# A fourth block-sum step in the later gate-and-up pairs of a two-layer encoder trunk

## The chip, the cores and the metric

The kernel runs on one core of one Trainium2 chip. The metric is the device time of one execution in microseconds; the median of several runs is compared. The profile is one execution taken by the hardware profiler; its busy times, waits and starts are the basis of all that follows. TensorE is PE in the profile's lines (PEld its weight loads), VectorE is DVE, ScalarE is ACT, GpSimd is POOL and SyncE, which issues most loads, is SP.

## The reference, cut to what matters

The trunk has two layers on 256 tokens of 2048 features, all in float32. Layer 0 mixes tokens by grouped-query attention, layer 1 by a recurrent block (a projection, a short convolution, two gated linear recurrences and an output projection). Each layer ends in the same feed-forward part:

```
x = x + mixer(rmsnorm(x))
x = x + swiglu(rmsnorm(x))
swiglu(h) = (silu(h @ w_gate) * (h @ w_up)) @ w_down     # w_gate, w_up: 2048 x 5632, w_down: 5632 x 2048
```

## The kernel before

**Matmuls in three passes.** Every float32 weight tile is split into two parts, `hi` (a rounded copy, by ScalarE, L141) and `lo` (the rest, by VectorE, L143), and so are the activations. A product is three matmuls: hi x hi, hi x lo, lo x hi. The tokens are the stationary operand (128 at a time), and 512 weight columns stream past them. A half is one load of 512 KB: two blocks of 128 input features by 512 output columns. Loads (`load_half`) use five buffers each for `raw`, `hi` and `lo`.

**Feed-forward order.** The 5632 hidden features of a layer are worked in eleven units of 512, called gate-and-up pairs here: a pair computes 512 columns of gate and of up at the same time. The eleven pairs come in three parts of 3, 4 and 4 (`PARTS`, in blocks of 128); after each part the down projection of its hidden features is added to the token-major residual `x_tok`, in two stages of two groups of 512 columns each. A pair has 2048 / 256 = 8 steps. A plain step loads one half for gate and one for up and does 8 products, 24 matmuls.

**Block-sum steps.** In some steps (`THREE` = 1, 3, 5; in the first pair of a layer 3 and 5) the 2 x 2 block product (two token blocks, two feature blocks, two column groups) is done with seven products, 21 matmuls, instead of eight, in the manner of Strassen and Winograd. It needs sums of weight blocks and of token blocks. `seven_forms` makes those of the weights: one half is loaded and split as always; a second transfer on POOL's queue writes the other half to `sr` and a third adds a part to it in flight (`fetch_next`, two buffers, each chain started when the buffer comes free); `wx` (256 KB, on SP's queue, one buffer) is a fourth. VectorE forms the sums in place (L320, L324, L325), ScalarE casts them (L322, L323, L327) and VectorE makes the low parts (L326, L328, L329). `x_forms` makes the token sums: for the layer's input once per step number (tiles `nf1`, `nf3`, `nf5`), and for the hidden features once per part (`hf0` to `hf2`). Four products go to PSUM tiles of their own (`p1`, `q5`, `q6`, `q7`, pool `pm`, four buffers); after the last block-sum step `merge` combines them into `g` and `u` in SBUF (tiles `fg`, `fu`). The other products go to the four ordinary accumulators (`acc`, four buffers).

**The order in a pair.** `unit_plan` and `pair_plan` write it: up to and including the last block-sum step, gate and up go together step by step; the remaining steps first for gate, then for up. When gate's last product is done, VectorE adds the accumulators to `g` (L848) and ScalarE applies silu; when up's is done, VectorE adds them to `u` (L851) and multiplies (L852). Then `u` is turned from token-major to feature-major: VectorE transposes 32 x 32 blocks (L865), ScalarE makes 16 small copies that put the blocks in place (L871, four calls of `copies`, four copies in each), and one cast (L878) and one subtraction (L879) split the result.

**What sets the order of the work.** TensorE's instructions run in the order written. For the other engines a scheduler of the framework decides, under order rules that the program adds: `in_line` keeps the weight work of ScalarE and of VectorE in the order of loading; `follow` puts one instruction behind another; `not_after` with `settled` says that an instruction must stand before the weight subtraction of the third half from then. The turning is not written out where it arises: its pieces go into a list `owed`, and `settle(n)` takes n pieces out at a given step, up to three at a block-sum step and one or two at a half of a plain one.

**The first gates.** In the recurrent mixer the projection is done in groups of 128 columns, and the gates of a block of 256 features are matmuls put between them by a clock: `later(delay, ...)` runs a piece once `delay` steps have gone by (a step is three matmuls of 256 columns there). `WHEN_FIRST` has the delays for block 0: its four gates at 24, 30, 36 and 42. A gate needs the split convolution output `xs` (L439, L440), reads weights `ghi` and `glo`, and then issues the weight load of the gate four places later (`load_gates`: a load on SP's queue, a cast on ScalarE, a subtraction on POOL).

Of the kernel before, what the change touches and what calls it, by code (L numbers as in the profile page):

```python
# [12 lines left out]
F32 = mybir.dt.float32  # L13
F32R = mybir.dt.float32r
AF = mybir.ActivationFunctionType
ALU = mybir.AluOpType
AX = mybir.AxisListType

P = 128
S = 256  # L20
D = 2048
KT = D // P
# [4 lines left out]
DFF = 5632  # L27
PARTS = [12, 16, 16]
THREE, TWO, SHORT = (1, 3, 5), (2, 5), 6
READY = 6  # L30
FIRST_STEPS = (0, 1, 2, 4, 3, 6, 5, 7)
HALF = 8
# [2 lines left out]
FOUR = WIDE // P  # L35
# [14 lines left out]
VALUES = (62, 98)  # L50
GATE_BUFS = 4
WHEN = (18, 25, 32, 39, 42, 46, 50, 54, 58, 60, 62, 64, 66, 70, 74)
WHEN_FIRST = (24, 30, 36, 42) + WHEN[4:]
WHEN_LAST = (5, 9, 13, 17, 19, 20, 21, 24, 24, 25, 26, 27, 33, 39, 39)

PK = {}
# [14 lines left out]
def trunk(ctx, tc, w, out):  # L71
    nc = tc.nc
    act, dve, pool, pe, sync = nc.scalar, nc.vector, nc.gpsimd, nc.tensor, nc.sync
# [13 lines left out]
    def nm(s):  # L87
        uid[0] += 1
        return f"{s}_{uid[0]}"
# [28 lines left out]
    def not_after(i, ahead=3, eng="dve"):  # L118
        due.setdefault((taken[0] + ahead, eng), []).append(i)
# [36 lines left out]
        return [(n, (0, 1)) for n in steps[:together]] + [(n, (j,)) for j in range(2) for n in steps[together:]]  # L156

    def unit_seven(i):
        return THREE[1:] if i == 0 else THREE

    def unit_plan(i):
        steps = range(KT // 2) if i else FIRST_STEPS
        return pair_plan(steps, 1 + steps.index(unit_seven(i)[-1]))

    def down_plan(n, alone):
# [36 lines left out]
    steps = range(KT // 2)  # L202
# [88 lines left out]
    owed = []  # L291

    def settle(n=1):
        while owed and n:
            owed.pop(0)()
            n -= 1
# [49 lines left out]
    def project_pair(xs, forms, plan, middle, done, ready=None):  # L346
        banks = [[], []]
        begun = set()

        def bank(j, a):  # L350
            while len(banks[j]) <= a:
                banks[j].append(new_acc())
            return banks[j][a]

        def product(acc, x, wt, last=False):
            for i, (a, b) in enumerate(((x[0], wt[0]), (x[0], wt[1]), (x[1], wt[0]))):
                pe.matmul(acc, a, b, start=id(acc) not in begun, stop=last and i == 2)  # L357
                begun.add(id(acc))
            step()
            step()  # L360

        def tokens(k, a):
            return [xs[k][:, o + a * P : o + (a + 1) * P] for o in (0, S)]

        seven = [n for n, cols in plan if n in forms]
        for i, (n, cols) in enumerate(plan):
            if n in forms:
                s1, s2, s3, s4 = forms[n]
                b11, b21, t3, b22, t1, t2, t4 = seven_forms()
                settle(3)  # L370
                if n == seven[0]:
                    p1, q6, q5, q7 = (ps_m.tile([P, WIDE], F32, tag="pm", name=nm("pm")) for _ in range(4))
                last = n == seven[-1]
                product(p1, tokens(2 * n, 0), b11, last)
                product(bank(0, 0), tokens(2 * n + 1, 0), b21)
                product(bank(1, 0), s4, b22)
                product(q7, s3, t3, last)
                product(q5, s1, t1, last)
                product(q6, s2, t2, last)
                product(bank(0, 1), tokens(2 * n + 1, 1), t4)  # L380
                if last:
                    middle(p1, q5, q6, q7)
                continue
            if len(cols) == 1 and i and len(plan[i - 1][1]) == 2:
                settle(-1)
                if ready:
                    ready()
            end = n == plan[-1][0]
            for j in cols:
                half()  # L390
                if i:
                    settle(2 if len(owed) > 6 else 1)
                hi, lo = (flat(t) for t in newest["tiles"])
                for a in range(2):
                    for k in range(2):
                        product(bank(j, a), tokens(2 * n + k, a), (hi[:, k, :], lo[:, k, :]), end and k == 1)
                if end:
                    done(j, banks[j])

    def merge(p1, q5, q6, q7):  # L400
        g, u = (fp[1].tile([P, 2, WIDE], F32, tag=t, name=nm(t), bufs=1) for t in ("fg", "fu"))
        act.copy(g[:, 0, :], p1)
        dve.tensor_tensor(g[:, 1, :], q6, g[:, 0, :], ALU.subtract)
        dve.tensor_tensor(u[:, 0, :], q5, g[:, 1, :], ALU.add)
        dve.tensor_tensor(g[:, 1, :], q7, g[:, 1, :], ALU.subtract)
        dve.tensor_tensor(u[:, 1, :], u[:, 0, :], q7, ALU.subtract)
        return g, u

    def three(o, hi, lo, x, start, stop):
# [56 lines left out]
    class Norm:  # L466
# [18 lines left out]
        def add(self, c):  # L485
            last = c == NCOL - 1
            parts = []
            fields = {}

            def first():  # L490
                for a in range(2):
                    act.activation(tmp("nj", (P, WIDE), mybir.dt.bfloat16, 1), x_tok[:, a, c, :], AF.Square, accum_out=self.sums[:, a, c : c + 1])
                if last and self.seven:
                    self.finish()
                fields["b"] = fp[0].tile([P, 2, FOUR, P], F32, tag="tb", name=nm("tb"))
                fields["f"] = fp[0].tile([P, 8, FOUR, 32], F32, tag="tf", name=nm("tf"))
                for a in range(2):
                    dve.transpose(fields["b"][:, a, :, :], x_tok[:, a, c, :])

# [50 lines left out]
    fp = []  # L550
# [285 lines left out]
    def ffn(norm, nxt):  # L836
# [4 lines left out]
        def unit(hid, hid_units, forms, parts, i):  # L841
# [19 lines left out]
            kept = {}  # L861

            def transposes():
                kept["b"], kept["f"] = (fp[0].tile([P, 2 * FOUR, P], F32, tag=n, name=nm(n), bufs=1) for n in ("tb", "tf"))
                dve.transpose(kept["b"], got[1])  # L865

            def copies(q):
                b = kept["b"][:].rearrange("p (a i) (k t) -> p a i k t", a=2, k=FOUR)
                f = kept["f"][:].rearrange("p q (k t) -> p q k t", k=FOUR)
                for i in range(4):  # L870
                    n = act.copy(f[32 * i : 32 * i + 32, q::4, :, :], b[32 * q : 32 * q + 32, :, i, :, :])  # L871
                    follow(n, line["act"])

            def split_tiles():
                f = kept["f"][:].rearrange("p q (k t) -> p k q t", k=FOUR)
                h = act_tiles()
                hi, lo = (h[:, :, o : o + S].rearrange("p k (q t) -> p k q t", t=32) for o in (0, S))
                act.copy(hi, f)  # L878
                dve.tensor_tensor(lo, f, hi.bitcast(F32), ALU.subtract)  # L879
                hid.extend(h[:, k, :] for k in range(FOUR))  # L880
                for k, n in enumerate(THREE):
                    if n in down_seven(parts // 2, False) and first <= 2 * n < len(hid):
                        forms[n] = x_forms(hid[2 * n], hid[2 * n + 1], f"hf{k}")

            owed.extend([transposes, *(partial(copies, q) for q in range(4)), split_tiles])

        line.update(act=None, dve=None)
        for p, n in enumerate(PARTS):
# [238 lines left out]
```

## Time and profile before

| | |
|---|---|
| median of 3 runs | 1963.46 us (1961.83 to 1963.49) |
| the profiled execution | 1964.66 us, span 1962.8 us |
| TensorE matmuls | 9641, busy 1955.2 us |
| VectorE busy | 1737.4 us (89%) |
| ScalarE busy | 1357.9 us (69%) |
| GpSimd busy | 233.7 us (12%) |
| loads from device memory | 431.02 MB, 221 GB/s over the span |
| mean granted TensorE clock | 0.998 |

Matmuls overlap in the pipe, so the mean length of one (389 ns for 512 columns) is longer than the distance from one start to the next; the distance is what counts for a sum. Operations of VectorE that follow one another overlap a little too, and there too the distance of starts is the price. A row of the timeline gives start, length, engine, line and operation, and how often; in square brackets stands how long the engine was idle before it and who released it. A row of the chain of waits gives start, length and what ran. A row of the windows gives, for a stretch, each engine's busy time and count, the granted clock, the share of the DMA engines and GB/s.

### The profile page before, as it was taken

What the parts mean: (1) busy time and instruction counts of PE and PEld (TensorE: products, weight loads), DVE (VectorE), ACT (ScalarE), POOL (GpSimd) and SP (SyncE); (2) the same over time, 40 slices, a digit from 0 to 9 for tenths busy, and PEclk for the clock granted to TensorE, in tenths of its full rate; (3) what the DMA queues carried; (4) which work ended last, traced back from release to release, by engine and by line L of the source; (5) the groups of instructions that cost most, each with busy time, mean ns of one, the idle gap of its engine ahead of it and who ended that gap; (6) DMA issues with size and microseconds to landing.
All of it is one profiled execution on the core that took longest, in us unless ns stands there. A gap on an engine that the chain in (4) does not pass through costs nothing.

```text
span 1962.8 us, 27715 instructions
## 1 busy us (share of the span) xinstructions
PE 1955.2 (100%) x9641; PEld 1659.9 (85%) x9641; DVE 1737.4 (89%) x2374; ACT 1357.9 (69%) x2075; POOL 233.7 (12%) x333
## 2 busy tenths in 40 slices
PE   9999999999999999999999999999999999999999
PEld 8888888888888888888899998888888888888887
DVE  6777889999999989999778986999998999989997
ACT  6666767665677556777689986767756776567763
POOL 0011000010011100101034331001101010011010
PEclk9999999999999999999999999999999999999999
DMA  8544667687677876776545556567767777777784
GB/s 333 186 147 138 202 204 240 219 258 246 209 246 242 269 245 214 228 234 232 197 166 184 190 166 209 193 203 243 245 233 239 240 240 255 229 245 236 234 261 163
DMA packets 136364, 434.95 MB, mean 222 GB/s; under 512 B 15264, under 2 KB 16160, under 8 KB 135968
## 3 DMA queue, kind: packets, MB, share of 16 engines
q1 hardware_dynamic: 109296, 360.01, 53.3%
q0 software_dynamic: 26784, 73.15, 14.7%
q8 instruction: 76, 1.25, 0.3%
q14 instruction: 64, 0.52, 0.1%
q10 hardware_dynamic: 144, 0.02, 0.0%
HBM read 431.02 MB, written 2.10 MB: 221 GB/s over the span
## 4 chain that ended last, share of the span: by engine, by line
PE 96%; ACT 2%; DVE 1%; issue 1%; DMA 0%; DVEq 0%; ACTq 0%
PE acc L357 60%; PE pm L357 12%; PE acc L273 10%; PE acc L410 3%; PE acc L411 3%; PE acc L412 3%; PE pm L273 1%; PE pm L411 1%; PE pm L412 1%; PE pm L410 1%; ACT tf L871 1%; DVE lo L143 1%; PE pm L748 1%; PE pm L780 1%; PE pm L766 0%
## 5 line engine op out<-in xcount | busy, mean ns | idle before, releaser
L143 DVE TENSOR_TENSOR lo<-raw,hi 128x1024 fp32r<-128x1024 f32 (+1 forms) x613 | 736.7, 1227 | 87.8 <-ACT hi L141 81.9
L141 ACT CAST hi<-raw 128x1024 fp32r<-128x1024 f32 (+1 forms) x613 | 627.4, 1046 | 255.3 <-PE acc L357 93.0
L357 PE MATMUL acc<-hi,xg 128*128 128x512 f32 x1920 | 612.9, 389 | 0.0
L357 PEld LDWEIGHTS acc<-hi,xg 128*128 128x128 f32 x1920 | 360.4, 188 | 74.7
L357 PE MATMUL acc<-hi,act 128*128 128x512 f32 x1258 | 402.1, 390 | 0.8 <-DVE act L879 0.5
L357 PE MATMUL acc<-lo,xg 128*128 128x512 f32 x960 | 373.5, 389 | 0.0
L357 PEld LDWEIGHTS acc<-hi,act 128*128 128x128 f32 x1258 | 236.0, 188 | 50.6 <-DVE act L879 1.4
L357 PE MATMUL acc<-lo,act 128*128 128x512 f32 x629 | 244.8, 389 | 0.0
L357 PEld LDWEIGHTS acc<-lo,xg 128*128 128x128 f32 x960 | 180.2, 188 | 37.5
L327 ACT CAST wxh<-raw 128x1024 fp32r<-128x1024 f32 x93 | 97.8, 1052 | 110.8 <-DVE raw L325 110.8
L871 ACT COPY tf<-tb 32x256 f32<-32x256 f32 x352 | 142.0, 404 | 5.5 <-DVE tb L865 1.6
L410 PE MATMUL acc<-xg,hi 128*128 128x256 f32 x512 | 145.6, 284 | 0.0
L411 PE MATMUL acc<-xg,hi 128*128 128x256 f32 x512 | 145.4, 284 | 0.0
L412 PE MATMUL acc<-xg,lo 128*128 128x256 f32 x512 | 145.2, 284 | 0.0
L357 PEld LDWEIGHTS acc<-lo,act 128*128 128x128 f32 x629 | 118.2, 188 | 23.8
L323 ACT CAST wxh<-wx 128x512 fp32r<-128x512 f32 x93 | 57.7, 621 | 110.4 <-DVE wx L320 78.2
L322 ACT CAST hi<-sr 128x1024 fp32r<-128x1024 f32 x93 | 97.7, 1051 | 39.2 <-PE acc L357 28.4
L329 DVE TENSOR_TENSOR wxl<-raw,wxh 128x1024 fp32r<-128x1024 f32 x93 | 112.7, 1211 | 6.9 <-ACT wxh L327 6.9
L326 DVE TENSOR_TENSOR lo<-sr,hi 128x1024 fp32r<-128x1024 f32 x93 | 113.1, 1216 | 0.0
L305 POOL DMA_DIRECT2D sr<-in_w_up_dram x64 | 35.6, 557 | 651.0 <-DVE lo L326 482.6
L273 PE MATMUL acc<-hi,xg 128*128 128x512 f32 x320 | 109.0, 401 | 0.3 <-ACT hi L141 0.3
L410 PEld LDWEIGHTS acc<-xg,hi 128*128 128x128 f32 x512 | 98.7, 193 | 0.0
(212 smaller groups left out, 3330.4 us busy)
## 6 DMA issues: line engine op xcount, KB each, us to landing
raw<-in_w_gate_dram SPq DMA_DIRECT2D x176, 512.0 KB, 5.4
raw<-in_w_down_dram SPq DMA_DIRECT2D x147, 512.0 KB, 5.5
raw<-in_w_up_dram SPq DMA_DIRECT2D x112, 512.0 KB, 5.6
sr<-in_w_up_dram POOLq DMA_DIRECT2D x64, 512.0 KB, 4.9
raw<-in_w_in_dram SPq DMA_DIRECT2D x64, 512.0 KB, 4.3
raw<-in_w_qkv_dram SPq DMA_DIRECT2D x46, 512.0 KB, 4.4
raw<-in_w_o_dram SPq DMA_DIRECT2D x32, 512.0 KB, 3.5
wx<-in_w_up_dram SPq DMA_DIRECT2D x64, 256.0 KB, 4.7
```

Source lines behind the costliest of these rows:

```text
L141: newest["cast"] = in_line("act", act.copy(hi[:, sl, :], raw[:, sl, :]))
L143: rest = in_line("dve", dve.tensor_tensor(lo[:, sl, :], raw[:, sl, :], hi[:, sl, :].bitcast(F32), ALU.subtract))
L273: pe.matmul(accs[a], x, wt[:, k, :], start=(k0 + k == 0 and n == 0), stop=(end and k == 1 and n == 2))
L322: in_line("act", act.copy(hi, raw))
L326: settled(in_line("dve", dve.tensor_tensor(lo, raw, hi[:].bitcast(F32), ALU.subtract)), taken[0] - 1)
L327: in_line("act", act.copy(xh[:, 1:, :], r1))
L329: in_line("dve", dve.tensor_tensor(xl[:, 1:, :], r1, xh[:, 1:, :].bitcast(F32), ALU.subtract))
L357: pe.matmul(acc, a, b, start=id(acc) not in begun, stop=last and i == 2)
L410: pe.matmul(o, hi, x[:, :S], start=start, stop=False)
L411: pe.matmul(o, hi, x[:, S:], start=False, stop=False)
L412: pe.matmul(o, lo, x[:, :S], start=False, stop=stop)
L871: n = act.copy(f[32 * i : 32 * i + 32, q::4, :, :], b[32 * q : 32 * q + 32, :, i, :, :])
```

## The change

Pairs 1 to 3 of a layer keep their plans. In pairs 4 to 11 a fourth step, number 6, becomes a block-sum step, and the order of the steps is new: 3, 0, 5, 2, 1, 4, 6, 7, with block-sum steps at the first, third, fifth and seventh place. Only step 7 is then left to be done for gate and for up apart. In a pair whose first step is a block-sum step, its two products into the second and third accumulator (`bank(0, 1)`, `bank(1, 0)`) come last. The token sums for step 6 (`nf6`) are made once per layer, after the turning of pair 2, as a further owed piece, that is during pair 3.

At a block-sum step one owed piece is given out, not three (none if the step is the first of its plan, three if it is the second), so the turning's copies come four at a time.

To make room for `nf6` the separate tile `tf` for the turned blocks is dropped: within a pair the copies go into the memory of the pair's own gate tile, and in the norms they go into a tile with the tag `fg`. The last subtraction of `merge` gets the order rule `not_after`. The first four gates of block 0 move from steps 24, 30, 36, 42 to 32, 38, 44, 50.

```diff
+MORE = (3, 5, 1, 6)
+LATER_STEPS = (3, 0, 5, 2, 1, 4, 6, 7)
-WHEN_FIRST = (24, 30, 36, 42) + WHEN[4:]
+WHEN_FIRST = (32, 38, 44, 50) + WHEN[4:]
...
     def unit_seven(i):
-        return THREE[1:] if i == 0 else THREE
+        return THREE[1:] if i == 0 else THREE if i < 3 else MORE
 
     def unit_plan(i):
-        steps = range(KT // 2) if i else FIRST_STEPS
+        steps = FIRST_STEPS if i == 0 else tuple(range(KT // 2)) if i < 3 else LATER_STEPS
         return pair_plan(steps, 1 + steps.index(unit_seven(i)[-1]))
...
-                settle(3)
+                settle((0, 3)[i] if i < 2 else 1)
...
                 product(p1, tokens(2 * n, 0), b11, last)
-                product(bank(0, 0), tokens(2 * n + 1, 0), b21)
-                product(bank(1, 0), s4, b22)
+                first = [(bank(0, 0), tokens(2 * n + 1, 0), b21)]
+                rest = [(bank(0, 1), tokens(2 * n + 1, 1), t4), (bank(1, 0), s4, b22)] if n == plan[0][0] else []
+                for t in first if rest else first + [(bank(1, 0), s4, b22)]:
+                    product(*t)
                 product(q7, s3, t3, last)
                 product(q5, s1, t1, last)
                 product(q6, s2, t2, last)
-                product(bank(0, 1), tokens(2 * n + 1, 1), t4)
+                for t in rest or [(bank(0, 1), tokens(2 * n + 1, 1), t4)]:
+                    product(*t)
...
-        dve.tensor_tensor(u[:, 1, :], u[:, 0, :], q7, ALU.subtract)
+        not_after(dve.tensor_tensor(u[:, 1, :], u[:, 0, :], q7, ALU.subtract))
...
-                fields["f"] = fp[0].tile([P, 8, FOUR, 32], F32, tag="tf", name=nm("tf"))
+                fields["f"] = fp[1].tile([P, 8, FOUR, 32], F32, tag="fg", name=nm("fg"), bufs=1)
...
-                kept["b"], kept["f"] = (fp[0].tile([P, 2 * FOUR, P], F32, tag=n, name=nm(n), bufs=1) for n in ("tb", "tf"))
+                kept["b"] = fp[0].tile([P, 2 * FOUR, P], F32, tag="tb", name=nm("tb"), bufs=1)
+                kept["f"] = got[0][:].rearrange("p a (q t) -> p (a q) t", t=P)
...
+            def last_form():
+                n = MORE[-1]
+                norm.forms[n] = x_forms(norm.xs[2 * n], norm.xs[2 * n + 1], f"nf{n}")
+
+            if i == 1:
+                owed.append(last_form)
```

More of the change, by code (lines that the diff above doesn't have):

```diff
@@ L868, in copies @@
                 b = kept["b"][:].rearrange("p (a i) (k t) -> p a i k t", a=2, k=FOUR)
-                f = kept["f"][:].rearrange("p q (k t) -> p q k t", k=FOUR)
+                f = kept["f"].rearrange("p q (k t) -> p q k t", k=FOUR)
                 for i in range(4):
@@ L874, in split_tiles @@
             def split_tiles():
-                f = kept["f"][:].rearrange("p q (k t) -> p k q t", k=FOUR)
+                f = kept["f"].rearrange("p q (k t) -> p k q t", k=FOUR)
                 h = act_tiles()
```

## The prediction

> **What bounds the kernel now.** I read the page first, then the busy time of each engine over the gate-and-up pairs and down stages of one part, then the vector engine's order in time, the chain of waits, and last the place where the first gates run.
>
> ```profile
> span 1962.8 us, 27715 instructions
> PE 1955.2 (100%) x9641; PEld 1659.9 (85%) x9641; DVE 1737.4 (89%) x2374; ACT 1357.9 (69%) x2075; POOL 233.7 (12%) x333
> GB/s 333 186 147 138 202 204 240 219 258 246 209 246 242 269 245 214 228 234 232 197 166 184 190 166 209 193 203 243 245 233 239 240 240 255 229 245 236 234 261 163
> PE 96%; ACT 2%; DVE 1%; issue 1%; DMA 0%; DVEq 0%; ACTq 0%
> ```
>
> The chain that ended last is TensorE for 96% of the span: TensorE sets the time today. A matmul taken away is worth its pitch if nothing else becomes late. The pitch is read from the chain of waits in order of time (start, length, matmuls). With two of its rows I show two of VectorE's timeline: the last weight operation (L329) of the third block-sum step, in the first and in the third pair of the second part of layer 0.
>
> ```profile
> 471.64 1.22 DVE L329 TENSOR_TENSOR wxl<-raw,wxh 128x1024 fp32r<-128x1024 f32 x1
> 479.48 17.00 PE acc L357 x75
> 559.72 1.22 DVE L329 TENSOR_TENSOR wxl<-raw,wxh 128x1024 fp32r<-128x1024 f32 x1
> 562.44 17.00 PE acc L357 x75
> ```
>
> 75 matmuls of 512 columns take 17.00 us, 0.2267 us each. The row at 479.48 begins with the last product of that step; the product before it (three matmuls, 0.68 us earlier, at 478.80) is the first that needs L329's output, finished at 472.86. So VectorE leads TensorE by 5.9 us at the end of the first pair. At the end of the third pair the same lead is 561.76 - 560.94 = 0.8 us. VectorE is nearly late already. The windows, one per pair and then two per down stage, say why:
>
> ```profile
> core 0: us, PE busy (x) PEld busy (x) DVE busy (x) ACT busy (x) POOL busy (x), PEclk, DMA share, GB/s
> 449.50:491.00 41.50, 41.50 (x185) 34.38 (x184) 37.22 (x43) 23.32 (x26) 4.25 (x6) 1.00 0.77 253
> 491.00:532.50 41.50, 41.50 (x185) 34.38 (x184) 38.07 (x49) 29.90 (x43) 4.24 (x6) 1.00 0.73 231
> 532.50:574.00 41.50, 41.50 (x185) 34.38 (x184) 39.66 (x51) 30.14 (x44) 4.24 (x6) 1.00 0.76 241
> 574.00:615.50 41.50, 41.50 (x184) 34.38 (x184) 39.66 (x51) 30.14 (x44) 4.24 (x6) 1.00 0.75 242
> 615.50:657.00 41.50, 41.50 (x184) 34.36 (x184) 39.51 (x47) 28.16 (x40) 4.26 (x6) 1.00 0.75 238
> 657.00:698.50 41.50, 41.50 (x184) 34.36 (x183) 38.25 (x46) 22.06 (x24) 4.25 (x6) 1.00 0.75 250
> ```
>
> A pair has 183 matmuls (five plain steps of 24, three block-sum steps of 21): 41.49 us. VectorE is busy 39.66 us of that in the third and fourth pair. The 1.8 us that it is idle are these:
>
> ```profile
> 540.95 6.63 ACT L871 COPY tf<-tb 32x256 f32<-32x256 f32 x16
> 548.26 0.69 DVE L328 TENSOR_TENSOR wxl<-wx,wxh 128x512 fp32r<-128x512 f32 x1 [1.51 <-ACT wxh L323]
> 549.21 1.23 DVE L329 TENSOR_TENSOR wxl<-raw,wxh 128x1024 fp32r<-128x1024 f32 x1 [0.26 <-ACT wxh L327]
> ```
>
> ScalarE runs the turning's 16 copies in one piece and VectorE waits 1.51 + 0.26 us behind it.
>
> **Part one: the fourth block-sum step.** It takes two plain halves (24 matmuls) and makes them 21. Eight pairs in each of two layers: 16 x 3 x 0.2267 = 10.9 us off TensorE, 0.68 a pair, which then needs 180 x 0.2267 = 40.8 us. The price on VectorE, from starts that follow one another without a gap:
>
> ```profile
> 535.48 0.68 DVE L325 TENSOR_TENSOR raw<-raw 128x512 f32<-128x512 f32 x1
> 536.08 1.21 DVE L326 TENSOR_TENSOR lo<-sr,hi 128x1024 fp32r<-128x1024 f32 x1
> 537.22 0.68 DVE L328 TENSOR_TENSOR wxl<-wx,wxh 128x512 fp32r<-128x512 f32 x1
> 537.82 1.23 DVE L865 STREAM_TRANSPOSE tb<-fu 128x1024 f32<-128x1024 f32 x1
> 538.98 1.18 DVE L329 TENSOR_TENSOR wxl<-raw,wxh 128x1024 fp32r<-128x1024 f32 x1
> 540.09 3.48 DVE L143 TENSOR_TENSOR lo<-raw,hi 128x1024 fp32r<-128x1024 f32 x3
> 543.49 0.68 DVE L320 TENSOR_TENSOR wx<-wx,raw 128x512 f32<-128x512 f32 x1
> ```
>
> A 512-element operation costs 0.60 us (535.48 to 536.08), a 1024-element one 1.13 (three from 540.09 to 543.49). A block-sum step has four of the first (L320, L324, L325, L328) and three of the second (L143, L326, L329): 5.8 us, where two plain halves cost 2.27. So +3.54 us of VectorE per pair, for 0.68 us saved on TensorE. The pairs in the steady part then want 39.66 + 3.54 = 43.2 us of VectorE in 40.8 us of TensorE: 2.4 us too much. The first pair of a part (37.22 + 3.54 = 40.8) is even.
>
> Sum over one part. VectorE enters the second pair with at most 5.9 us of lead. Three pairs lose 3 x 2.4 = 7.2, so 1.3 us of stall is the least. It is more, because the lead does not fall evenly. Of a pair's 39.66 us, 10 x 1.13 + 3 x 5.8 = 28.7 are weights; the other 10.9 are merges, sums, activation products, turning and forms, and I choose to put two thirds (7.3) into the stretch around the pair's end, where everything from the merge to the transposition lies. In the new order block-sum steps sit at positions 1, 3, 5, 7 of 8, so the stretch from the last one to the next pair's first holds one plain step only: 45 matmuls, 10.2 us, against 8.1 of weights and 7.3 of the rest: the lead drops 5.2 there. The three other stretches gain 10.2 - 8.1 = 2.1 each, less the remaining 3.6: +2.7. From 5.9: 0.7 after the first border, 3.4, a stall of 1.8 at the second, 2.7, a stall of 2.5 at the third. 4.3 us a part, between 1.3 and, if the two thirds are all, some 6. Four parts: 17.2 (5 to 24). A second way to see it: the six windows hold 232.4 us of VectorE in 249.0; the change makes that 232.4 + 4 x 3.54 = 246.5 in 249.0 - 2.7 = 246.3 of TensorE, so whatever VectorE is still idle in a part (16.6 us now, 4.7 by this sum and the next term) lengthens it.
>
> ScalarE gets these more per step, the other two casts replacing plain ones:
>
> ```profile
> L327 ACT CAST wxh<-raw 128x1024 fp32r<-128x1024 f32 x93 | 97.8, 1052 | 110.8 <-DVE raw L325 110.8
> L323 ACT CAST wxh<-wx 128x512 fp32r<-128x512 f32 x93 | 57.7, 621 | 110.4 <-DVE wx L320 78.2
> sr<-in_w_up_dram POOLq DMA_DIRECT2D x64, 512.0 KB, 4.9
> sr<-in_w_up_dram POOLq DMA_DIRECT2D x64, 256.0 KB, 7.1
> ```
>
> 1.67 us on 30.14 leaves ScalarE at 31.8 of 40.8: no bound by itself. Each step also loads 1.5 MB (raw 512 KB, wx 256, sr 512 + 256) where the plain one loads 1.0, 257 GB/s in a pair of 40.8 us, inside the slices of 258 and 269 that the page shows; the chained fetch of sr on POOL's queue needs 4.9 + 7.1 = 12 us and a buffer comes round every 20.4. The wx load is on SP's queue ahead of later weights, as now. I cost all DMA at nothing; its cover is that lead, and where the lead is zero a late load shows at once.
>
> **Part two: copies four at a time.** Sixteen copies take 6.63 us, four take 1.66, so ScalarE's weight casts wait at most that and VectorE's 1.77 us per pair can go. What is late next is VectorE's own work. I leave 0.2 us of it a pair: 4 parts x 0.6 = 2.4 us (0 to 21, the end where all 1.77 stay in three pairs of four parts).
>
> **Part three: copies land in the old gate tile.** The merge's first copy of the next pair must now wait for the split (L879) of the last. The split is given out at position 5, the merge stands behind position 7: 10.2 us apart, nothing. The new order rule on the merge's last subtraction puts it ahead of a weight subtraction on VectorE; behind that are all further weights, but TensorE waits for those PSUM banks too. Nothing, or some tenths either way.
>
> **Part four: the fourth form,** once a layer, in pair 3 (still three steps, with a lead as in the table's third row):
>
> ```profile
> L338 DVE TENSOR_TENSOR tb<-xg 128x256 f32<-128x256 f32 x12 | 4.7, 418 | 0.0
> L340 DVE TENSOR_TENSOR tb<-tb 128x128 f32<-128x128 f32 x88 | 23.4, 282 | 0.2
> L343 DVE TENSOR_TENSOR nf<-tb,nf 128x512 fp32r<-128x512 f32 x6 | 4.1, 683 | 0.0
> ```
>
> 2 x 0.42 + 4 x 0.28 + 0.68 = 2.6 us against some 1.8 of idle and 0.8 of lead: 0.9 each, +1.8 (0 to 5).
>
> **Part five: the first gates 8 steps later.**
>
> ```profile
> 970.40:974.40 4.00, 2.19 (x9) 1.32 (x9) 3.92 (x10) 1.51 (x2) 0.13 (x2) 0.83 0.76 294
> 974.40:979.70 5.30, 5.30 (x27) 5.30 (x27) 1.20 (x3) 3.70 (x6) 1.52 (x3) 0.50 0.36 115
> 979.70:985.00 5.30, 5.30 (x45) 5.30 (x45) 2.15 (x4) 3.79 (x9) 1.30 (x1) 0.98 0.16 49
> ...
> 970.45 0.28 PE L412 MATMUL acc<-xg,lo 128*128 128x256 f32 x1
> 973.25 0.58 PE L410 MATMUL pm<-xs,ghi 128*128 128x256 f32 x1 [0.93 <-DVE xs L439]
> ...
> 971.36 0.41 DVE L440 TENSOR_TENSOR xs<-xc,xs 128x256 fp32r<-128x256 f32 x1
> 972.91 0.28 DVE L439 CAST xs<-xc 128x256 fp32r<-128x256 f32 x1
> 973.50 0.41 DVE L440 TENSOR_TENSOR xs<-xc,xs 128x256 fp32r<-128x256 f32 x1
> ```
>
> The first gate is due at 970.6 and its last operand is done at 973.9; TensorE stands, and the granted clock falls to 0.50 until 979.7. 36 matmuls in 9.3 us, where 0.118 each (45 in 5.30) makes 4.25: 5.0 us lost. Eight steps are 24 matmuls, 2.8 us, of weights already split (the buffers are five halves): the gate comes at 973.4, when all but one operand is there. I take 4.5 us back (2.2, if half the loss returns, to 5.0). With each gate move its next weight load on SP's queue, ScalarE's cast and POOL's subtraction; they are wanted a block later.
>
> [...]
>
> **Sum.** -10.9 + 17.2 + 2.4 + 1.8 - 4.5 = +6.0. The profiled execution is 1964.66 us (span 1962.8, 1.86 around it), 1.2 above the median of 1963.46: 1970.7 for such a run, 1969.5 as a median. Own range 1962 to 1977.
>
> **Rivals.**
> (A) The lead carries: it falls evenly, the stall is its least (1.3 a part), copies and the form cost nothing, the gates bring 4.9. -10.9 + 5.2 - 4.9 = -10.6: 1953. For it: most of the 16.6 us that VectorE is idle in a part is order and not work, and the change reorders. Against: it would leave VectorE idle 1.1 us a part, and the steady pairs have 1.8 us to give where 3.54 + 0.68 are asked. It decides from a stall of 1.8 a part down, where even the forecast's other terms leave -10.9 + 7.2 + 2.4 + 1.8 - 4.5 = -4.0.
> (B) ScalarE's waits stay as they are, 1.77 x 12 = 21 us in place of 2.4, because scheduled copies still bunch, and the form costs all 5: -10.9 + 17.2 + 21 + 5 - 4.5 = +28: 1991. For: VectorE now has no lead left, so every such wait reaches TensorE. Against: pieces of four.
> (C) Stalls at the borders bring the half clock with them, as at 974.4: 5.3 us at 0.50 lose 2.65, at two borders of four parts 21 us, less what VectorE catches up meanwhile, about half: +16: 1980. For: the row at 974.40. Against: there TensorE worked 2.19 of 4.00 us; a stall of 2.5 in a border stretch of 10.2 is thinner. [...]
>
> **Numbers.** Forecast 0.50, A 0.28, B 0.12, C 0.10. About 0.2% (3.9 us) is what a measurement of this kernel tells from no change: faster is below 1959.5, slower above 1967.4. The forecast gives 0.03 faster, 0.14 same, 0.33 slower; A 0.25 and 0.03; B and C 0.22 slower less 0.01. Faster 0.28, same 0.18, slower 0.54. A's own range is 1949 to 1959; the range 1951 to 1986 leaves out its lowest end and most of B.
>
> **What would show it.** Right: VectorE busy 99% in the second to fourth pair of each part, TensorE idle released by VectorE's L326, L328 or L329 at pair borders, pair lengths of 40.8, 41, 42.8 and 43.5 us; no half clock near 970 and the stage about 4.5 us shorter. The forecast is wrong if those pairs all last 40.8 us (A), if VectorE's waits on ScalarE's casts remain (B), or if the clock row shows less than 1.00 in them (C).

## The result, and the profile after

The changed kernel takes 2063.79 us (median of 4 runs, 2061.48 to 2066.51) where the kernel before takes 1962.64: ratio 1.0522, 95% interval 1.0509 to 1.0534. It is 101 us slower; the forecast was 1969.5 and the range ended at 1986. The profiled execution took 2064.38 us. The head of its page, and its chain that ended last:

```profile
span 2062.6 us, 27849 instructions
PE 1989.1 (96%) x9593; PEld 1657.1 (80%) x9593; DVE 1797.5 (87%) x2468; ACT 1390.3 (67%) x2113; POOL 257.4 (12%) x365
PE 62%; DVE 18%; ACT 10%; issue 8%; DMA 3%; POOL 0%; SPq 0%; DVEq 0%; ACTq 0%; POOLq 0%
```

TensorE has 48 matmuls fewer, as planned, but its share of the chain fell from 96% to 62%: 28% is now VectorE's and ScalarE's, and 8% is "issue", time in which the engine waited for nothing that the profile shows. Where the time went, the stages say (us, from the first matmul of a stage to the first of the next; layer 0 / layer 1):

| stage | before | after | difference |
|---|---|---|---|
| pairs 1 to 3 | 125.1 / 125.1 | 125.5 / 125.5 | +0.8 |
| first down stage | 63.1 / 63.1 | 69.2 / 68.2 | +11.2 |
| pairs 4 to 7 | 165.9 / 165.9 | 187.5 / 185.3 | +40.9 |
| pairs 8 to 11 | 166.7 / 165.9 | 187.4 / 186.1 | +40.8 |
| later down stages | 168.0 / 166.1 | 168.7 / 166.9 | +1.6 |
| recurrence, its output projection | 323.1 | 327.9 | +4.8 |

Nearly all is in the four later parts, as pairs 4 to 7 and 8 to 11 of the two layers are called here. Two pairs in steady state there, by windows from transposition to transposition:

```profile
core 0: us, PE busy (x) PEld busy (x) DVE busy (x) ACT busy (x) POOL busy (x), PEclk, DMA share, GB/s
505.36:553.91 48.55, 44.21 (x183) 34.77 (x182) 43.33 (x56) 31.87 (x45) 5.66 (x8) 0.96 0.71 213
553.91:602.46 48.55, 43.98 (x183) 34.38 (x182) 43.34 (x57) 31.82 (x45) 5.67 (x8) 0.96 0.72 220
```

A pair lasts 48.55 us: 43.3 of VectorE's work, which is the 43.2 the prediction had, and 5.2 in which it waits, where the prediction left 0.2. The timeline shows the wait. VectorE's rows come first, then ScalarE's:

```profile
553.91 1.24 DVE L871 STREAM_TRANSPOSE tb<-fu 128x1024 f32<-128x1024 f32 x1
555.07 0.65 DVE L327 TENSOR_TENSOR raw<-raw 128x512 f32<-128x512 f32 x1
555.64 1.21 DVE L328 TENSOR_TENSOR lo<-sr,hi 128x1024 fp32r<-128x1024 f32 x1
556.77 0.68 DVE L330 TENSOR_TENSOR wxl<-wx,wxh 128x512 fp32r<-128x512 f32 x1
558.00 1.23 DVE L331 TENSOR_TENSOR wxl<-raw,wxh 128x1024 fp32r<-128x1024 f32 x1 [0.54 <-ACT wxh L329]
560.75 1.22 DVE L145 TENSOR_TENSOR lo<-raw,hi 128x1024 fp32r<-128x1024 f32 x1 [1.53 <-ACT hi L143]
563.50 1.23 DVE L145 TENSOR_TENSOR lo<-raw,hi 128x1024 fp32r<-128x1024 f32 x1 [1.52 <-ACT hi L143]
566.25 1.23 DVE L145 TENSOR_TENSOR lo<-raw,hi 128x1024 fp32r<-128x1024 f32 x1 [1.52 <-ACT hi L143]
```

```profile
552.17 0.62 ACT L325 CAST wxh<-wx 128x512 fp32r<-128x512 f32 x1 [4.42 <-PE acc L359]
555.24 1.65 ACT L877 COPY fg<-tb 32x256 f32<-32x256 f32 x4 [2.44 <-DVE tb L871]
556.91 1.05 ACT L329 CAST wxh<-raw 128x1024 fp32r<-128x1024 f32 x1
557.99 1.66 ACT L877 COPY fg<-tb 32x256 f32<-32x256 f32 x4
559.67 1.05 ACT L143 CAST hi<-raw 128x1024 fp32r<-128x1024 f32 x1
```

Four copies now stand ahead of each of the four weight casts behind the transposition. ScalarE needs 1.65 + 1.05 = 2.70 us for a half, VectorE has one subtraction of its own to do meanwhile, some 1.2 us, and waits for the difference: 1.5 us, three times a pair, and 0.54 once: 5.1 us. Meanwhile ScalarE itself stood idle for 2.44 us for the transposition it was about to copy, and 4.42 us before that. The kernel before had the copies behind five large casts, where VectorE had 5.8 us of its own from their start (540.95, until its L326 ends at 546.76), and it waited 1.77. Kernel before, ScalarE's casts ahead of the copies, then VectorE's last operation ahead of its wait:

```profile
536.19 1.05 ACT L327 CAST wxh<-raw 128x1024 fp32r<-128x1024 f32 x1 [3.10 <-DVE raw L325]
537.14 2.95 ACT L141 CAST hi<-raw 128x1024 fp32r<-128x1024 f32 x3
540.00 1.04 ACT L322 CAST hi<-sr 128x1024 fp32r<-128x1024 f32 x1
...
545.54 1.22 DVE L326 TENSOR_TENSOR lo<-sr,hi 128x1024 fp32r<-128x1024 f32 x1
```

### The profile page after: what moved, and what is told of

It reads as the page before. It is cut to its first block, busy times and chain, and to the rows that moved or that the text cites. A ratio compares the mean times of both kernels' runs of the same rounds, so it can differ in the third digit from the quotient of the medians.

```text
span 2062.6 us, 27849 instructions
## 1 busy us (share of the span) xinstructions
PE 1989.1 (96%) x9593; PEld 1657.1 (80%) x9593; DVE 1797.5 (87%) x2468; ACT 1390.3 (67%) x2113; POOL 257.4 (12%) x365
## 4 chain that ended last, share of the span: by engine, by line
PE 62%; DVE 18%; ACT 10%; issue 8%; DMA 3%; POOL 0%; SPq 0%; DVEq 0%; ACTq 0%; POOLq 0%
PE acc L359 35%; PE acc L275 9%; PE pm L359 8%; DVE lo L145 5%; ACT fg L877 5%; PE acc L415 2%; PE acc L416 2%; PE acc L417 2%; DVE lo L328 2%; DVE raw L326 1%; DMA wx<-in_w_up_dram 1%; ACT hi L143 1%; DVE wx L322 1%; DVE wxl L331 1%; PE pm L275 1%
## 5 line engine op out<-in xcount | busy, mean ns | idle before, releaser
L145 DVE TENSOR_TENSOR lo<-raw,hi 128x1024 fp32r<-128x1024 f32 (+1 forms) x597 | 716.3, 1227 | 144.9 <-ACT hi L143 143.9
L143 ACT CAST hi<-raw 128x1024 fp32r<-128x1024 f32 (+1 forms) x597 | 606.6, 1044 | 180.4 <-PE acc L359 50.7
L359 PE MATMUL acc<-hi,xg 128*128 128x512 f32 x1696 | 550.3, 390 | 0.7
L359 PEld LDWEIGHTS acc<-hi,xg 128*128 128x128 f32 x1696 | 318.5, 188 | 71.4 <-ACT hi L143 5.9
L359 PE MATMUL acc<-lo,xg 128*128 128x512 f32 x848 | 332.0, 391 | 9.1 <-DVE lo L145 9.1
L359 PEld LDWEIGHTS acc<-lo,xg 128*128 128x128 f32 x848 | 159.1, 188 | 48.3 <-DVE lo L145 14.9
L877 ACT COPY fg<-tb 32x256 f32<-32x256 f32 x352 | 142.1, 404 | 35.5 <-DVE tb L871 31.2
L331 DVE TENSOR_TENSOR wxl<-raw,wxh 128x1024 fp32r<-128x1024 f32 x109 | 132.7, 1217 | 9.6 <-ACT wxh L329 9.6
L307 POOL DMA_DIRECT2D sr<-in_w_up_dram x80 | 44.4, 556 | 637.6 <-DVE lo L328 395.5
L359 PE MATMUL pm<-wxh,nf 128*128 128x512 f32 x320 | 119.1, 414 | 0.0
L308 POOL DMA_DIRECT2D sr<-in_w_up_dram x80 | 69.1, 863 | 365.7 <-DMA sr<-in_w_up_dram 306.4
```

What stands on the lines that cost most here:

```text
L143: newest["cast"] = in_line("act", act.copy(hi[:, sl, :], raw[:, sl, :]))
L145: rest = in_line("dve", dve.tensor_tensor(lo[:, sl, :], raw[:, sl, :], hi[:, sl, :].bitcast(F32), ALU.subtract))
L331: in_line("dve", dve.tensor_tensor(xl[:, 1:, :], r1, xh[:, 1:, :].bitcast(F32), ALU.subtract))
```

## The experiments

The times in brackets are of the kernel before on the same chip. Where one run is given, the effects told are far larger than the spread of the medians above.

**Copies left out.** The changed kernel without twelve of the sixteen copies at the three pair borders of each later part (so it does not compute the trunk any more). It is one test in `copies`:

```diff
+                if few and q:     # few: pairs 4 to 6 and 8 to 10
+                    return
```

> The changed kernel, with 12 of the 16 small copies of the turning left out (so not computed) after the first, second and third pair of the second and third part of each layer. Theory S: a steady pair lasts 48.5 us because ScalarE now runs four copies (1.65 us) between one weight cast and the next and VectorE waits 1.5 us three times and 0.5 once, 5.1 us a pair, on top of 43.2 us of its own work. Then the steady pairs fall to 43.3 to 44 us and the kernel to about 2005 us (12 pairs by 4.6 to 5.1 us). Rival V: VectorE's added work and the new places of the block-sum steps make the pair long whatever ScalarE does; then it stays at 47 us or more and the kernel within 15 us of 2064. In no case do the pairs reach TensorE's 40.8 us.

Measured 1995.71 us (1961.48). The four later parts fall from 185.3 to 187.5 down to 169.0, 169.2, 169.0 and 169.5, by 69.5 us in all. In steady state VectorE is then the bound and hardly waits:

```profile
517.00:560.50 43.50, 42.25 (x182) 33.35 (x181) 42.93 (x56) 26.65 (x35) 5.67 (x8) 1.00 0.79 244
```

So of the 81.7 us lost in the parts, 69.5 go with the copies as long as the fourth step is there, and 12.3 (some 3 a part) are left for the fourth step and its order. That split depends on what is taken out first, because both draw on the same spare time of VectorE: with the copies kept and the fourth step taken out (three steps, below) the parts get only 27 us back. The size fits in the main: three pair borders a part, each with 5.1 - 0.54 us less to wait, make 13.7 of the 17.4 a part; where the other 3.7 come from was not traced. Counted from TensorE's first matmul of a pair to that of the next, the four pairs of a part last 40.8, 41.1 to 41.7, 43.5 to 43.6 and 43.5 to 43.8 us here; in the changed kernel they last 40.8, 46.2 to 49.8, 48.2 to 50.1 and 48.3 to 49.8.

**Is it the pieces, or their place?** Four copies, then twelve in one run at the same place:

```diff
-                settle((0, 3)[i] if i < 2 else 1)
+                settle((0, 3)[i] if i < 2 else 3)
```

> The changed kernel, but the turning's copies in pairs 5 to 11 are given out as four and then twelve in one run, at the same place: ahead of the same weight casts. Theory P (place: what costs is that the copies stand between casts where VectorE has only one subtraction of its own per cast, so it waits for 16 copies less what it has to do, 5.1 us a pair): nothing changes, 2055 to 2068, the long parts stay at 184 to 188 us, VectorE waits once for some 4.5 us where it waited three times for 1.5. Theory N (it is the giving out in pieces that costs; in one run the wait falls back to the 1.8 us it had): parts of 173 to 177, 2010 to 2025.

Measured 2058.56 us (1960.82), parts of 185.1 to 185.9: theory P. VectorE's and ScalarE's rows:

```profile
561.31 3.50 DVE L145 TENSOR_TENSOR lo<-raw,hi 128x1024 fp32r<-128x1024 f32 x3 [4.83 <-ACT hi L143]
...
555.25 4.96 ACT L877 COPY fg<-tb 32x256 f32<-32x256 f32 x12
```

One wait of 4.83 us instead of three of 1.5: cutting the run in pieces neither helped nor hurt.

**The copies a block-sum step later.** All sixteen are taken out inside `seven_forms` of the next block-sum step (the fifth in the plan), behind its cast of `sr` and in the order of the weight casts:

```diff
+    def seven_forms(between=0):
...
         in_line("act", act.copy(hi, raw))
+        settle(between)     # 4 at the third block-sum step of a four-step pair
...
-                    n = act.copy(...)
-                    follow(n, line["act"])
+                    in_line("act", act.copy(...))
```

> The changed kernel, but in pairs 5 to 7 and 9 to 11 the 16 copies stand in one run one block-sum step later, behind that step's four large casts and ahead of its two small ones: there VectorE has about 6.3 us of operations of its own that need no new cast (3 x 1.13 + 4 x 0.60 + 0.5), against 6.6 us of copies and a cast of 0.62. Theory P (place): the wait falls from 5.1 us a pair to between 0.5 and 1.8, so parts of 170 to 175 us where they are 185 to 188 now, and 2000 to 2020 in all. Rival L (VectorE, with no lead left, waits for most of the 16 copies wherever they stand): parts stay above 180, 2040 or more.

Measured 2077.15 us (1960.82), and yet the parts are right: 174.7, 174.7, 175.5 and 174.7, where the changed kernel has 185 to 187. What VectorE waits in a pair, beside the run of copies:

```profile
526.35 1.22 DVE L329 TENSOR_TENSOR lo<-sr,hi 128x1024 fp32r<-128x1024 f32 x1
530.20 0.69 DVE L331 TENSOR_TENSOR wxl<-wx,wxh 128x512 fp32r<-128x512 f32 x1 [2.63 <-ACT wxh L326]
531.15 1.22 DVE L332 TENSOR_TENSOR wxl<-raw,wxh 128x1024 fp32r<-128x1024 f32 x1 [0.26 <-ACT wxh L330]
...
522.88 6.64 ACT L879 COPY fg<-tb 32x256 f32<-32x256 f32 x16
```

2.9 us instead of 5.1, for the same sixteen copies; I had expected 0.5 to 1.8, but from the start of the copies VectorE has only 4.7 us of its own here (522.88 to 527.57). The total rose because my edit put all turning copies into the forced order, in the other stages too: pairs 1 to 3 took 138.3 and 138.9 us, the later down stages 9 more each. I take it for the same cost, in stages that the change had left alone; the next run takes the forced order out of them again.

**The same, only in the later pairs, and the fourth form early.** The forced order only where pairs 5 to 7 and 9 to 11 take the copies; the form as in the run described below:

> The changed kernel with its four steps, but the copies in pairs 5 to 7 and 9 to 11 in one run a block-sum step later (only there, so that the early pairs and the down stages stay as in the changed kernel), and the fourth form made right after pair 1. If the costs add up as read from the single runs: 2064 less 4 x 12.3 for the parts (187 to 174.7, as in the run with the copies a step later) less 9 to 12 for the early form: 2000 to 2008, and the down stages back at 83.4 and 85.4, the first pairs at 125.5. Rival X (the +9 in the down stages and the +13 in the first pairs of that run came from the later copies in the pairs before them, not from the forced order inside them): down stages of 90 or more stay, 2025 or more.

Measured 2016.67 us (1961.34). The parts are 174.7 to 175.0, pairs 1 to 3 are back at 125.5 and the first down stages at 64.1, as expected. The later down stages keep 2.6 to 3.4 us each of the 9, so the total is 9 us above the upper end of what I expected; why those stay was not followed up.

**Three steps, the rest as changed.**

```diff
-MORE = (3, 5, 1, 6)
+MORE = (3, 5, 1)
```

> The changed kernel without its fourth block-sum step: pairs 4 to 11 keep three (the steps 3, 5 and 1, in the new order), the copies are given out as in the changed kernel, no fourth form is made. VectorE's work falls by 3.5 us a pair to some 39.7, TensorE's rises to 41.5. Theory P (the copies' waits stand beside VectorE's work, both drawing on the same spare time): 39.7 + 5.1 = 44.8 us a pair in steady state, 3.3 over TensorE, three times a part, less the 5.9 us of lead at its start: parts of 170 to 177 us, 1985 to 2010. Rival F (without the fourth step VectorE has room enough, the waits are hidden again): parts of 166 to 168, 1962 to 1975.

Measured 2023.91 us (1961.34), parts of 177.7 to 180.8: 54 us more than before, without a single matmul saved or a fourth step paid. Rival F falls; theory P's mechanism holds, but its sizes were too low: its parts by up to 4 us, its total by 14. VectorE's first cycle is 45.3 us (L145 after its first 1.53 us wait starts at 503.67 and at 549.00), near 39.7 + 5.1. The next two are longer: its transpositions lie 45.4, 46.6 and 48.2 us apart, and in the last two of these stretches it also waits 1.4 us for the cast of the hidden features' token sums (`hf`).

**Three steps in the old order, pieces.** The kernel before with one word changed:

```diff
-                settle(3)
+                settle(1)
```

> The kernel before, with three block-sum steps, its order and its tiles, but with one piece of turning given out at a block-sum step, not three: the copies then stand as eight, four and four between the casts. Theory P: VectorE has work of its own during the eight, and at the other two waits some 1.5 us, as much as the 1.8 us it waits before the change; same within 0.3%: 1957 to 1969. Rival N (each piece put between two casts costs 1.5 us, and there is no lead in the later pairs): 3 us a pair in the 12 pairs with turning, less the 1.8 that goes: +14, 1977.

Measured 1985.40 us (1960.82): above theory P's 1969 and nearer to the rival's 1977, but not by the rival's mechanism. The later parts are 0.5 to 1.5 us longer, 3.7 in all, as theory P had it: here the first eight copies still stand behind the five large casts. What both theories left out are the first down stages, 8.7 and 8.9 us longer: the copies are cut 8 and 8 by the step's last two casts (L323, L327), not 8, 4 and 4 as expected, and the turned operand comes late for the down stage that reads it. TensorE's waits there:

```profile
PE acc L357 <- ACT act L878: 3.4, 1, 3.4
PE acc L357 <- DVE act L879: 2.1, 1, 2.1
```

**The fourth form made right after pair 1**, not with the owed work of pair 2:

```diff
-                n = THREE[0]
-                norm.forms[n] = x_forms(...)
+                for n in (THREE[0], MORE[-1]):
+                    norm.forms[n] = x_forms(...)
```

> The changed kernel, with the token sums of step 6 made right after pair 1, where those of step 1 are made, and not during pair 3. If those sums pushed pair 3's turning late, and with it the first down stage (69.2 and 68.2 us in the changed kernel against 63.1 before), the down stages return to 63 to 64 us and the kernel gains 9 to 12 us. Rival: the down stages are long because of the new memory for the turned blocks (the merge waits for the split); then they stay at 68 to 69 us.

Measured 2051.50 us (1961.48). The first down stages fall from 69.2 and 68.2 to 64.1 each, 9.3 us. In the changed kernel the form's operations stand ahead of pair 3's transposition, which starts at 396.31 instead of 391.49, and TensorE waits in the down stage for the operand turned after it (VectorE's timeline and TensorE's waits, changed kernel):

```profile
393.44 0.69 DVE L345 TENSOR_TENSOR nf<-tb,nf 128x512 fp32r<-128x512 f32 x1
...
396.31 1.24 DVE L871 STREAM_TRANSPOSE tb<-fu 128x1024 f32<-128x1024 f32 x1
```

```profile
PE acc L359 <- DVE act L885: 1.3, 1, 1.3
PE acc L359 <- ACT act L884: 1.1, 1, 1.1
```

The 64.1 us that stay are 1 us more than before in each layer. That is not the form's: the run with three steps makes no fourth form, and its first down stages are 64.1 us too. Its cause was not looked for.

**The norm's turned blocks in the gate tile**, alone on the kernel before:

```diff
-                fields["f"] = fp[0].tile(..., tag="tf", ...)
+                fields["f"] = fp[1].tile(..., tag="fg", ...)
```

> The kernel before, with one edit: the norms' turned blocks go into a tile with the tag fg, as in the changed kernel. Theory M: the first gate weights are then loaded some 50 us later, about when the recurrent stage starts, its weights are cast after them, and the stage grows by 3 to 8 us (gates still at their old steps, so it waits longer than the changed kernel did). Rival G: memory is not the matter; the time stays within 1.5 us of before.

Measured 1965.17 us, ratio 1.0020 (1.0010 to 1.0029); the recurrence is 3.2 us longer. The queue that loads the gate weights, and TensorE, in that run:

```profile
SPq L940 <- DVE xg L480: 5.7, 1, 5.7
...
PE pm L410 <- ACT hi L141: 3.7, 1, 3.7
```

By these waits, the gate weights' memory is that of the feed-forward tiles. Before, the first load waited for the last use of `fg` in the down stage (`x_tok` L586, 4.2 us); with the norm's blocks in `fg` it waits for the norm's last split, and the loads, their casts and a weight cast behind these come late.

The changed kernel has this tile and the later gates together, and there the stall at the first gate did not go. TensorE in its windows around that gate:

```profile
1023.00:1029.00 6.00, 3.33 (x13) 0.76 0.74 251
1029.00:1035.00 6.00, 6.00 (x38) 0.67 0.45 138
```

51 matmuls in 12 us, where 0.118 each makes 6.0: some 6 us lost, where the kernel before lost 5.0. The first gate load is issued 8 us into the recurrence (1007.12); in the kernel before it is issued 45 us ahead of it (904.94).

**The first gates.** Three sets of delays on the kernel before:

```diff
-WHEN_FIRST = (24, 30, 36, 42) + WHEN[4:]
+WHEN_FIRST = (32, 38, 44, 50) + WHEN[4:]     # gates alone, as in the change
+WHEN_FIRST = (28, 33, 38, 42) + WHEN[4:]     # half way
+WHEN_FIRST = (32, 36, 40, 42) + WHEN[4:]     # late, but ahead of the decays at 42
```

> The kernel before, with only the first gates 8 steps later. Theory M (gate weights came late in the changed kernel because their tiles lie on memory that is free only after the last norm operand): here they are loaded early as before, the first gates stop waiting, the half clock near 970 is gone and the time falls by 3.5 to 5 us. Rival G: the later gates themselves lengthen the stage (the pieces behind them come late), and it is 2 to 4 us slower than before, as the recurrent stage of the changed kernel was (+3.4 us).

Measured 1963.18 us, ratio 1.0007 (0.9997 to 1.0016). TensorE's work in two windows, before and then with the gates alone, and its waits in the recurrence and behind it, with the gates alone:

```profile
970.00:990.00 20.00, 18.19 (x124) 17.32 (x123) 12.10 (x22) 12.89 (x23) 6.76 (x12) 0.83 0.45 156
990.00:1010.00 20.00, 20.00 (x170) 20.00 (x169) 16.48 (x30) 18.85 (x31) 6.01 (x8) 1.00 0.50 174
```

```profile
970.00:990.00 20.00, 19.62 (x165) 19.42 (x164) 10.84 (x21) 17.84 (x29) 5.72 (x12) 1.00 0.47 153
990.00:1010.00 20.00, 18.54 (x155) 18.36 (x155) 15.03 (x28) 19.30 (x31) 8.11 (x9) 1.00 0.46 153
```

```profile
PE acc L410 <- DVE act L440: 2.0, 2, 1.5
PE acc L357 <- DVE gl L925: 1.8, 1, 1.8
```

The stall at the first gate is gone: 41 matmuls more, 4.8 us at 0.118 each. It comes back 20 us later, 15 matmuls fewer, and as 1.8 us at the end.

> The kernel before with the first block's four gates at the steps 28, 33, 38 and 42, none past the decays that begin at 42 (the change has 32, 38, 44, 50, so that two gates fall among the decays). In the run with the gates alone the stall at the first gate went (from 124 to 165 matmuls in 20 us) and came back as 1.5 us on the conv's output half a block later and 1.8 us on the last gelu. Theory O (the gates that fall among the decays push the first block's later work back): here half of the stall goes and nothing comes back: 2 to 4 us faster, 0.998 to 0.999. Theory T (what the gates give up is taken by the next block whatever the order): no difference, 0.9995 to 1.0005.

Measured 1958.67 us (11 runs; 1961.33), ratio 0.9988 (0.9979 to 0.9997); the recurrence takes 231.4 us where it took 235.4.

> The kernel before with the first block's gates at 32, 36, 40 and 42: the first as late as in the change, but all ahead of the decays at 42. Theory O: the whole of the 5 us at the first gate returns and at most 1 us comes back later: 4 to 5 us faster, 0.9975 to 0.998. Theory T: no difference, 0.9995 to 1.0005.

Measured 1958.02 us (11 runs; 1961.33), ratio 0.9982 (0.9974 to 0.9991); the recurrence takes 230.4.

```profile
970.00:990.00 20.00, 19.62 (x164) 19.42 (x164) 11.06 (x21) 17.40 (x32) 8.34 (x12) 1.00 0.49 158
990.00:1010.00 20.00, 20.00 (x170) 20.00 (x169) 19.09 (x34) 18.07 (x31) 6.94 (x8) 1.00 0.57 190
```

As theory O had it: with the first gate as late as in the change, but no gate among the decays, the stall goes and nothing comes back in the next window. Whether the place among the decays did the harm, or only that the later gates were later still (38, 44 and 50 against 36, 40 and 42), these runs do not separate. This version is some 3 us faster than the kernel before, a little under the 4 to 5 that I expected.

**Two of VectorE's operations to GpSimd.** With the copies a step later, the form early and the two tiles of the norm's turning exchanged, `wx<-wx,raw` (L322) and the low part of it (L331) become GpSimd's:

```diff
-        in_line("dve", dve.tensor_tensor(x, x, r1[:, 0, :], ALU.add))
+        pool.tensor_tensor(x, x, r1[:, 0, :], ALU.add)
...
-        in_line("dve", dve.tensor_tensor(xl[:, 0, :], x, ..., ALU.subtract))
+        pool.tensor_tensor(xl[:, 0, :], x, ..., ALU.subtract)
```

> The changed kernel with the copies a step later (as in the run of that name), the fourth form of the hidden state made right after pair 1, the norm's turning with its two tiles exchanged, and two of VectorE's four 512-element operations of each block-sum step (the first block sum and the low part of it) made by GpSimd: 0.60 us each off VectorE, some 1.6 us each on GpSimd, which is busy for 5.7 us of a pair. VectorE then has 43.2 - 8 x 0.60 = 38.4 us of work and up to 1.8 of waiting in a pair of 40.8 us of TensorE. Theory V (VectorE's sum is what holds the later pairs once the copies are out of the way): TensorE carries the pairs again, parts of 164 to 167 us, 1948 to 1962 in all. Rival G (GpSimd's operations come late behind its own transfers' waits, or take more than 1.6 us beside VectorE): parts above 170, 1985 or more.

Measured 2142.59 us (1960.82), parts of 185.6 to 195.4, where the copies a step later without this gave 174.7 to 175.5: rival G. (It carries the forced order in all stages, as above, worth some 60 us of it.) One such border shows both halves of that rival: VectorE's subtractions take longer (three 4.88 us, 3.48 elsewhere), and then it waits 2.48 us for GpSimd's sum. The last section has the rows.

## Why the prediction was wrong

It had the sign and the right engine, and missed the size by 94 us. Term by term:

- **TensorE, -10.9.** Right: 9641 matmuls before, 9593 after.
- **Part one, VectorE's price of the fourth step: +17.2 against the -10.9.** The mechanism was right: 3.5 us of VectorE a pair, a pair of 43.2 us of VectorE against 40.8 of TensorE, borders where TensorE waits. Net it said +6.3 over the four parts; with most of the copies out, +12.3 was measured. The signs it named came in that run: pairs of 40.8, 41, 42.8 and 43.5 us were forecast, 40.8, 41.1 to 41.7, 43.5 and 43.5 to 43.8 measured, with VectorE busy 98.7% in a steady pair. In the changed kernel itself VectorE is busy for 89%.
- **Part two, the copies, +2.4, range 0 to 21: the step that failed.** With three of the four pieces out the parts lose 69.5 us; without the fourth step the copies still cost 54. Two things in it were wrong. I wrote that a cast waits at most for one piece of 1.66 us and that the 1.77 us of before can go. Each piece does cost that little, but each stands before a different cast, and VectorE pays 1.5 us for each anew. And the range took the old wait, 1.77 us a pair, as the worst. That wait was only what was left after 5.8 us of VectorE's own work had covered the rest of the 6.63 us. The change moved the copies to where VectorE has no such work. The bound from above stood in the rows of the prediction: four copies and a cast are 2.7 us, a subtraction is 1.13, so up to 1.6 us for each of four pieces, 6.3 a pair, 75 us in three pairs of four parts.
- **Rivals B and C** were both on the way. What ScalarE's waits cost reaches TensorE, as B said, at three times B's price; but B's reason, that the copies still bunch, is not what happened: they were spread, and in one run at the same place they cost the same. At the three borders of one part the clock falls to between 0.50 and 0.58 after the stall, as C said (last section), but no run shows C's 16 us for it.
- **Part three, the tile `fg`, nothing.** The cover that I named, the distance from split to merge, holds inside the pairs. I did not ask who else waits for that tile once the norm uses it; the first gate loads do: +3.2.
- **Part four, the form, +1.8, range 0 to 5.** I priced its 2.6 us of VectorE against the idle time of pair 3. It stands ahead of the transposition, whose result the first down stage reads: +9.3 for the place.
- **Part five, the gates, -4.5.** With the gates alone moved, the stall went as forecast (4.8 us), but I looked only at the first gate. Two of the moved gates fall among the decays, the block's later work comes late, and all of it is given back; with the order kept, 3 us stay. In the changed kernel the stall did not even go: the gate loads came late, the clock row at the first gate still falls to 0.67, and the recurrence is 3.4 us longer, not 4.5 shorter.

The terms as measured: 69.5 + 12.3 for the later parts, 11.2 for the first down stages, 4.8 for recurrence and output projection, 2.4 for the rest of the feed-forward stages, -0.2 for the first stage: 100, which is the difference of the two spans.

## What to carry to other kernels

When a consumer engine is nearly full, price a helper's work by its place in the queue: ahead of which cast it stands, and how much of its own the consumer can do until that cast is done. The wait seen before is no upper bound for the wait after a move (here 1.77 us a pair before, 5.1 after); the helper's whole time, with the cast behind it, less the consumer's own work at the new place is. And whatever is moved or given a new tile has a second reader: ask, for each piece that becomes later, which stage behind it was waiting for its end.

## What the runs showed of the hardware

**The granted clock after a stall of 3.24 us, and after shorter ones.** The border of a pair in the changed kernel, TensorE alone (its longest idle stretch there is 3.24 us, until 523.88):

```profile
517.00:521.00 4.00, 3.65 (x17) 1.00 0.72 210
521.00:524.50 3.50, 0.62 (x2) 0.98 0.01 2
524.50:527.50 3.00, 3.00 (x8) 0.50 0.58 180
527.50:531.00 3.50, 3.50 (x16) 0.97 0.99 399
```

After 3.5 us with two matmuls, eight take 3.0 us at a granted clock of 0.50, where they would take 1.8 at 0.2267. At the next two borders of that part, after idle stretches of 3.24 and 3.25 us, it is 0.58 (573.00 to 576.00) and 0.50 (621.00 to 625.00). It does not show as time of its own there: VectorE's work and waits already fill the 48.55 us of the pair. In the first down stage, where the longest single wait is 1.3 us, the clock fell to 0.61 (changed kernel):

```profile
404.00:412.00 8.00, 4.81 (x17) 0.98 0.83 208
412.00:416.00 4.00, 4.00 (x12) 0.61 0.91 370
```

TensorE was idle for 3.2 us of the 8 there, in several short waits.

**Beside each other, GpSimd or VectorE took longer.** In the run with two operations on GpSimd, VectorE's three subtractions that start beside GpSimd's L331, and GpSimd's own L322 beside a run of VectorE's:

```profile
577.41 4.88 DVE L145 TENSOR_TENSOR lo<-raw,hi 128x1024 fp32r<-128x1024 f32 x3
...
577.35 1.58 POOL L331 TENSOR_TENSOR wxl<-wx,wxh 128x512 fp32r<-128x512 f32 x1
...
551.68 5.78 POOL L322 TENSOR_TENSOR wx<-wx,raw 128x512 f32<-128x512 f32 x1 [4.81 <-DMA wx<-in_w_up_dram]
...
552.83 3.48 DVE L145 TENSOR_TENSOR lo<-raw,hi 128x1024 fp32r<-128x1024 f32 x3
556.24 0.68 DVE L410 TENSOR_TENSOR fg<-pm,fg 128x512 f32<-128x512 f32 x1
...
583.45 1.29 POOL L322 TENSOR_TENSOR wx<-wx,raw 128x512 f32<-128x512 f32 x1 [4.52 <-issue]
...
584.77 0.69 DVE L327 TENSOR_TENSOR raw<-sr,raw 128x512 f32<-128x512 f32 x1 [2.48 <-POOL wx L322]
```

Three such subtractions take 3.48 us at 552.83; beside L331 they took 4.88, 1.4 more, about what L331 takes (1.58). L322 took 1.29 us at 583.45, while VectorE was idle, and 5.78 at 551.68; what held it there until 557.46 the rows do not show. VectorE's 218 operations fewer saved little: in the changed kernel the two lines took 149.4 us (74.7 each), but the five weight lines that VectorE kept took 132.7 us more, 1264.0 where the changed kernel has 1131.3; an L145 took 1336 ns on average where it was 1227.
